# A hybrid decoder layer on one core: five read-in transfers for the RWKV-7 inverse, its steps tied to a large product, its way back by products with identity columns, and small edits at both ends of the program

## The chip, the cores and the metric

The kernel runs on one core of one Trainium2 chip. The core has a matrix engine (TensorE, in the profile PE, with its weight loads as PEld), three engines for elementwise work (VectorE or DVE, ScalarE or ACT, GpSimd or POOL) and SyncE (SP), whose queue here issues most transfers. A name that ends in q (SPq, ACTq) is the engine's queue, at work on waiting and issuing. Each engine takes its instructions strictly in the order in which the program lists them. The metric is the time of one execution in microseconds of device time, smaller is better. Times inside an execution are counted from the start of its span.

## What is computed

One layer of an inference step, in float32, for 256 new tokens of one prompt and one new token each of 8 sampled sequences, so 264 columns in all, with model width 2048:

```
x = x + 0.5 * swiglu(rmsnorm(x, n1), f1g, f1u, f1d)      # width 5504
proj = rmsnorm(x, nm) @ w_in                             # 2048 -> 1536 + 3328
o_att  = sliding-window attention, 16 query heads, 4 kv heads, sinks, relative bias
o_rwkv = RWKV-7 time mixing, 16 heads of 64
x = x + concat(o_att, o_rwkv) @ w_out
x = x + 0.5 * swiglu(rmsnorm(x, n2), f2g, f2u, f2d)
y = rmsnorm(x, final_norm)
```

The outputs are y, the new key and value windows, the RWKV state and the shift columns. The RWKV recurrence over the prompt's tokens, per head, is

```
sa = S @ (-kk);  S = S * exp(logw) + sa (kk*a)^T + v k^T;  y = S @ r
```

The kernel does not step through the tokens. It cuts them into chunks of 64, and inside a chunk the dependence of each token on the earlier ones is a strictly lower triangular 64x64 system. Its inverse is put together from two 32x32 blocks on the diagonal and one product for the block beside them. The 32x32 inverses are what the change is mostly about.

## The kernel before

**Activations and weights.** Activations lie with features on partitions and the 264 tokens as columns. Every weight is loaded from memory in float32 in pieces of 128x512 (`chunk`, L116). ACT rounds a piece to a short float (`hi`, L123), DVE computes the rest (`lo`, L124), and each 128x128 block takes three products, hi with hi, hi with lo and lo with hi (`gemm`, L127, `mm`, L73). A piece is thus twelve large products. There are six raw buffers and four each of `hi` and `lo`.

**Stages.** `first_ffn` (L284), then `mixing_body` (L337), then `second_ffn` (L912). The FFNs are almost nothing but large products. Mixing first multiplies by w_in, 38 output tiles (`win`, L374) of four pieces, then runs the output projection in three passes (`PASS`, L895) of 16 tiles. The small work of attention and RWKV is written as generators in a list `tasks`. After each piece of a large product, `tick` (L78) advances every task by one `yield`. I call that a chunk step. `pause(n)` lets n chunk steps go by. An output pass begins with `drain` (L83), which finishes the tasks that it needs.

**What orders the queues.** The order in which the program is written is a priority, not the final order. A planner with its own estimates of durations and transfers puts the instructions of each engine into their final order: among those that it believes ready, the earliest written goes first. Weight pieces of mixing have a raised priority. A buffer that is asked for again is given out once its last reader is done.

**The RWKV batches.** The 16 heads are 8 pairs, in four batches of two pairs (`BATCH`). `prep` (L401) computes per pair the masked products (`gm`), and sends their diagonal 32x32 blocks to a scratch in memory (`sa`, L488). When both pairs of a batch are there, `chain` (L527) goes on:

1. Read-in (L538 to L541): the 32 matrices of a batch, spread over 128 partitions with four partitions for each, come in as `X` (each matrix whole, four copies of it, one transfer a copy) and `Y` (named Xt in the profile, each partition a quarter of the rows, one transfer a quarter). Partition g*32+r holds copy g of matrix r. There is one buffer each.
2. `pause(DWAIT)`, eight steps, four for the last batch.
3. Thirty steps of substitution on DVE (L546 to L553), each a multiplication into `st` and an addition into Xt, with a `yield` after every fourth.
4. POOL fills ones into the diagonal (L555).
5. Way back: Xt is written to a second scratch `sb` (four transfers, L557) and from there read into `TT` (four transfers, L562) in the layout of the products.
6. `pause(DWAIT)` again, then two DVE transposes make `TN` from the first diagonal block of each half (L567).
7. Two sets of small products with a copy on ACT after each (`zs`, L579, `TT`, L588) make the block beside the diagonal. Then follow the products and copies that lead to the state and the output (`W` and `uv`, L602 to L604, and on).

One `yield` stands between the steps of 7. The tasks of attention (`attend`, L732) run in the same stage, with exponentials and table loads on ACT.

**Start.** `first_ffn` loads the first column block of x with the norm gains (`x0`), then one and two further blocks on the ACT queue, then four at a time. `NWARM` products of ones run on PE from the first microsecond. The first part multiplies all eight accumulators by the first four blocks of x before it goes on.

**End.** The sum of squares of the last rows comes from two half sums, each by small products into a PSUM tile of its own (L934 to L937). ACT copies one, DVE adds the other (L940, L941), then come root, reciprocal, and a product that spreads the factors over the partitions (L945), with five products that only keep PE busy in between (`hot`). ACT copies the result for POOL (L947), and DVE and POOL multiply the 16 output tiles in groups, each followed by its store (L948 to L952).

Of the kernel before, what the change touches and what calls it, by code (L numbers as in the profile page):

```python
# [7 lines left out]
F32 = mybir.dt.float32  # L8
# [5 lines left out]
P = 128  # L14
# [33 lines left out]
def body(tc, I, O):  # L48
    nc = tc.nc
    V, A, G, TE, SP = nc.vector, nc.scalar, nc.gpsimd, nc.tensor, nc.sync  # L50
    cnt = [0]

    def uid(s):
# [19 lines left out]
    def mm(out, lhsT, rhs, start=True, stop=True, **k):  # L73
        TE.matmul(out, lhsT, rhs, start=start, stop=stop, **k)  # L74

# [19 lines left out]
    with ExitStack() as ctx:  # L95
# [30 lines left out]

        def gemm(ps, src, xs, step=None, rng=None, ahead=True):  # L127
            n = len(xs)
            for k0 in range(0, n, CH):
                k1 = min(n, k0 + CH)  # L130
                if rng and k0 not in rng:
                    continue
                hi, lo = chunk(src[:, k0 * P:k1 * P], k1 - k0, V, ahead)
                for k in range(k0, k1):
                    xh, xl = xs[k]
                    c = slice((k - k0) * P, (k - k0 + 1) * P)
                    mm(ps[:, :T], hi[:, c], xh, k == 0, False)
                    mm(ps[:, :T], hi[:, c], xl, False, False)
                    mm(ps[:, :T], lo[:, c], xh, False, k == n - 1)
                if step:  # L140
                    step()
# [67 lines left out]

        def ffn(nrm, xr, gu, dn, nxt, load, begin=None, side=None):  # L210
            rstd = None
            f0 = 0
            for pi, nf in enumerate(PARTS):
# [5 lines left out]
                if first:  # L219
                    banks = [acc() for _ in range(NACC)] + [mp() for _ in range(NM)]  # L220
                    n0 = len(banks) // 2
                    for k in range(CH):
                        at = load(k)
                    for k0 in range(0, KD, CH):
                        if begin and k0 + CH < KD:
                            begin(k0 // CH + 1)
                        xs = nrm.xs + [None] * (KD - len(nrm.xs))
                        for i, ps in enumerate(banks):
                            with tc.issue_after(at.ins) if begin and k0 == 0 < i else nullcontext():
                                gemm(ps, gu[i // 2, i % 2], xs, rng=(k0,), ahead=False)  # L230
                            if i >= len(banks) - CH and k0 + CH < KD:
                                load(k0 + CH + i - len(banks) + CH)
# [51 lines left out]
        def first_ffn(n2):  # L284
# [8 lines left out]
            with tc.tile_pool(name="f1", bufs=1) as fp:  # L293
# [14 lines left out]

                ffn(n1, xr, I["gu1"], I["dn1"], nxt, load, more)

# [26 lines left out]
        def mixing_body(mx, n2, n3, XD, XR):  # L337
# [31 lines left out]
            scr = [dp.tile([BATCH[b] * 16, 1024], F32, tag=f"sa{b}", name=f"sa{b}") for b in range(nbat)]  # L369
            scr2 = [dp.tile([BATCH[b] * 16, 1024], F32, tag=f"sb{b}", name=f"sb{b}") for b in range(nbat)]  # L370
            mixed = [None] * 16
# [155 lines left out]
            def chain(bt):  # L527
# [4 lines left out]
                ng = P // nr  # L532
                if ng == 3:
                    ng = 2
                nj = 32 // ng
                X = ring((ng * nr, 32, 32), "X", 1)
                Y = ring((ng * nr, nj, 32), "Xt", 1)
                for g in range(ng):  # L538
                    SP.dma_start(X[g * nr:(g + 1) * nr], scr[bt.i].rearrange("r (s t) -> r s t", s=32))
                    SP.dma_start(Y[g * nr:(g + 1) * nr],  # L540
                                 scr[bt.i].rearrange("r (j g t) -> g r j t", g=ng, t=32)[g])  # L541
# [4 lines left out]
                for s in range(1, 31):  # L546
                    m, w = -(-s // ng), 31 - s
                    t = ring((ng * nr, m, w), "st", 2)
                    shp = (ng * nr, m, w)
                    tt(V, t, bc(X[:, s:s + 1, s + 1:], shp), bc(Y[:, :m, s:s + 1], shp), ALU.mult)  # L550
                    tt(V, Y[:, :m, s + 1:], Y[:, :m, s + 1:], t, ALU.add)
                    if s % NSTEP == 0:
                        yield  # L553
                for g in range(ng):
                    G.memset(Y[g * nr:(g + 1) * nr].rearrange("p j t -> p (j t)")[:, g:g + (nj - 1) * (32 + ng) + 1:32 + ng], 1.0)  # L555
                for g in range(ng):
                    SP.dma_start(scr2[bt.i].rearrange("r (j g t) -> g r j t", g=ng, t=32)[g], Y[g * nr:(g + 1) * nr])  # L557
                yield from pause(1)
                for h in range(2):
                    for blk in range(2):  # L560
                        x = h * 64 + blk * 32
                        SP.dma_start(TT[x:x + 32, :, blk * 32:blk * 32 + 32],  # L562
                                     scr2[bt.i].rearrange("(h b m) (s t) -> h b s m t", h=2, b=2, s=32)[h, blk])
                yield from pause(DWAIT[bt.i])
                TN = ring((P, n * 4, 32), "TN", 1)
                for h in range(2):
                    V.transpose(TN[h * 64:h * 64 + 32], TT[h * 64:h * 64 + 32, :, 0:32])  # L567
                yield
# [343 lines left out]
        def second_ffn(n3, xr, XR):  # L912
# [6 lines left out]
            with tc.tile_pool(name="f2", bufs=1) as fp:  # L919
# [13 lines left out]
                p = fin.sums[0]  # L933
                sm, rp, hot = [mp(), mp()], mp(), mp()  # L934
                for m, q in zip(sm, p):
                    for j in range(3):
                        mm(m[0:88, j:j + 1], q[:, j * 88:j * 88 + 88], ones[:, 0:1])  # L937
                for _ in range(5):
                    mm(hot[:, :P], ones, p[1][:, :P])
                A.copy(rt[:, 3:6], sm[0][0:88, 0:3])  # L940
                tt(V, rt[:, 0:3], sm[1][0:88, 0:3], rt[:, 3:6], ALU.add)  # L941
                act(rt[:, 0:3], rt[:, 0:3], AF.Sqrt, scale=1.0 / D, bias=eps[0:88, 0:1])
                V.reciprocal(rt[:, 0:3], rt[:, 0:3])
                for j in range(3):
                    mm(rp[:, j * 88:j * 88 + 88], bc(rt[:, j:j + 1], (88, P)), C[0:88, CID:CID + 88])  # L945
                rb = tmp()
                A.copy(rb, rp[:, :T])  # L947
                for i, (e, o, n) in enumerate(((V, 0, 1), (V, 1, 1), (G, 2, 1), (V, 4, 4), (G, 3, 1), (V, 8, 4), (G, 14, 1), (V, 12, 2), (V, 15, 1))):  # L948
                    y = ys[o // 4][:, o % 4:o % 4 + n]
# [112 lines left out]
```

## Time and profile before

| what | us |
|---|---|
| median of three runs | 2013.53 (2012.96 to 2017.21) |
| profiled execution, its own time | 2014.05 |
| its span | 2012.1 |
| first FFN at full rate, 69 to 761 | 692.00 |
| mixing, 760 to 1191 | 431.00 |
| second FFN, 1303 to 2000 | 697.00 |
| from the last large product to the end, 2000 to 2012.1 | 12.10 |

The profile is of one execution. Its span is what lies between the first and the last instruction, and its time is 1.95 us more. In the rows, `out<-in` names tiles with buffer numbers left out; `128x512 f32` is partitions by elements; `L74` is the line of the helper `mm`, so PE's groups are told apart by their tiles. A bracket `[5.00 <-DMA ...]` is the time that the engine sat idle before an instruction and what ended it. Where a wait has several semaphores, the one that came last is named, which need not be the cause. Each product in float32 appears as two PE instructions.

### The profile page before, as it was taken

What the parts mean: (1) busy time and instruction counts of PE and PEld (TensorE: products, weight loads), DVE (VectorE), ACT (ScalarE), POOL (GpSimd) and SP (SyncE); (2) the same over time, 40 slices, a digit from 0 to 9 for tenths busy, and PEclk for the clock granted to TensorE, in tenths of its full rate; (3) what the DMA queues carried; (4) which work ended last, traced back from release to release, by engine and by line L of the source; (5) the groups of instructions that cost most, each with busy time, mean ns of one, the idle gap of its engine ahead of it and who ended that gap; (6) DMA issues with size and microseconds to landing.
All of it is one profiled execution on the core that took longest, in us unless ns stands there. A gap on an engine that the chain in (4) does not pass through costs nothing.

```text
span 2012.1 us, 45443 instructions
## 1 busy us (share of the span) xinstructions
PE 1990.5 (99%) x17088; PEld 1956.4 (97%) x17088; DVE 1306.4 (65%) x2576; ACT 1032.6 (51%) x2047; POOL 257.0 (13%) x368
## 2 busy tenths in 40 slices
PE   9999999999999999999998999999999999999998
PEld 9999999999999999999988889999999999999998
DVE  5865555655556577688777766776666666666665
ACT  5644444444444456655555654654444444444445
POOL 0401001010010222121200010120101001010012
PEclk9999999999999999999999999999999999999999
DMA  6565565655555566554555345565565665655554
GB/s 226 177 192 193 183 194 189 185 184 176 187 177 185 182 200 211 153 157 129 149 150 165 118 137 181 174 184 184 192 179 191 187 192 189 185 191 184 191 179 145
DMA packets 227708, 358.39 MB, mean 178 GB/s; under 512 B 42384, under 2 KB 81312, under 8 KB 227488
## 3 DMA queue, kind: packets, MB, share of 16 engines
q1 hardware_dynamic: 220896, 346.41, 55.0%
q10 hardware_dynamic: 6592, 9.08, 1.4%
q8 instruction: 134, 2.20, 0.4%
q14 instruction: 86, 0.70, 0.1%
HBM read 347.26 MB, written 10.21 MB: 178 GB/s over the span
## 4 chain that ended last, share of the span: by engine, by line
PE 94%; DMA 2%; DVE 2%; issue 1%; ACT 1%; SPq 1%; DVEq 0%; POOL 0%; ACTq 0%; POOLq 0%
PE acc L74 85%; PE m L74 8%; DMA sb<-Xt 1%; DVE lo L58 0%; DMA TT<-sb 0%; DMA xsp<-x 0%; DMA x<-in_x 0%; DMA Xt<-sa 0%; PE m L507 0%; ACT t L68 0%; DVE y L58 0%; DMA sa<-gm 0%; SPq L557 0%; ACT hi L123 0%; PE m L757 0%
## 5 line engine op out<-in xcount | busy, mean ns | idle before, releaser
L58 DVE TENSOR_TENSOR lo<-raw,hi 128x512 fp32r<-128x512 f32 (+1 forms) x1288 | 871.2, 680 | 547.9 <-ACT hi L123 521.1
L123 ACT CAST hi<-raw 128x512 fp32r<-128x512 f32 (+1 forms) x1288 | 777.1, 607 | 840.9 <-PE acc L74 762.3
L74 PE MATMUL acc<-s,hi 128*128 128x264 f32 x5940 | 1112.0, 287 | 0.9 <-ACT hi L123 0.9
L74 PEld LDWEIGHTS acc<-s,hi 128*128 128x128 f32 x5940 | 924.2, 189 | 6.7 <-issue 1.9
L74 PE MATMUL acc<-s,lo 128*128 128x264 f32 x2970 | 848.9, 286 | 4.1 <-DVE lo L58 3.9
L74 PEld LDWEIGHTS acc<-s,lo 128*128 128x128 f32 x2970 | 560.3, 189 | 8.0 <-DVE lo L58 5.4
L74 PE MATMUL acc<-t,hi 128*128 128x264 f32 x2752 | 502.6, 284 | 0.0
L74 PEld LDWEIGHTS acc<-t,hi 128*128 128x128 f32 x2752 | 426.0, 188 | 0.0
L74 PE MATMUL acc<-t,lo 128*128 128x264 f32 x1376 | 388.6, 284 | 0.0
L58 POOL TENSOR_TENSOR t<-t,t 128x264 f32<-128x264 f32 (+1 forms) x148 | 150.9, 1020 | 1148.3 <-ACT hi L123 790.8
L74 PEld LDWEIGHTS acc<-t,lo 128*128 128x128 f32 x1376 | 258.3, 188 | 0.0
L74 PE MATMUL acc<-y,hi 128*128 128x264 f32 x648 | 123.7, 284 | 0.0
L74 PEld LDWEIGHTS acc<-y,hi 128*128 128x128 f32 x648 | 100.9, 188 | 0.1
L74 PE MATMUL acc<-y,lo 128*128 128x264 f32 x324 | 91.7, 283 | 0.0
L58 DVE TENSOR_TENSOR t<-acc,t 128x264 f32<-128x264 f32 x156 | 67.4, 432 | 36.8 <-PE acc L74 36.5
L58 POOL TENSOR_TENSOR o<-o,o 128x264 f32<-128x264 f32 x43 | 36.4, 847 | 234.6 <-ACT o L68 228.9
L74 PE MATMUL acc<-o,hi 128*128 128x264 f32 x324 | 63.1, 285 | 0.0
L74 PEld LDWEIGHTS acc<-y,lo 128*128 128x128 f32 x324 | 61.0, 188 | 0.0
L61 DVE SCALAR_TENSOR_TENSOR s<-acc,s 128x264 f32<-128x264 f32 x96 | 40.6, 427 | 15.4 <-PE acc L74 14.9
L74 PEld LDWEIGHTS acc<-o,hi 128*128 128x128 f32 x324 | 50.3, 188 | 0.0
L74 PE MATMUL m<-s,hi 128*128 128x264 f32 x260 | 48.0, 284 | 0.0
L61 DVE SCALAR_TENSOR_TENSOR x<-acc,x 128x264 f32<-128x264 f32 x96 | 40.5, 426 | 9.8 <-PE acc L74 9.3
(249 smaller groups left out, 1278.8 us busy)
## 6 DMA issues: line engine op xcount, KB each, us to landing
raw<-in_gu SPq DMA_DIRECT2D x688, 256.0 KB, 3.3
raw<-in_dn SPq DMA_DIRECT2D x224, 256.0 KB, 2.8
raw<-in_win SPq DMA_DIRECT2D x152, 256.0 KB, 3.4
raw<-in_dn SPq DMA_DIRECT2D x160, 192.0 KB, 2.7
raw<-in_wout SPq DMA_DIRECT2D x64, 256.0 KB, 3.2
xsp<-x ACTq DMA_DIRECT2D x16, 132.0 KB, 3.7
s<-xsp SPq DMA_DIRECT2D x16, 132.0 KB, 4.2
ld<-in_sT SPq DMA_DIRECT2D x16, 128.0 KB, 3.5
```

The source lines that it names most:

```text
L58: return e.tensor_tensor(out=out, in0=a, in1=b, op=op)
L61: return V.scalar_tensor_tensor(out=out, in0=a, scalar=s, in1=b, op0=op0, op1=op1)
L74: TE.matmul(out, lhsT, rhs, start=start, stop=stop, **k)
L123: A.copy(hi[:, :w], raw[:, :w])
```

## The change

The read-in of `X` becomes one transfer that repeats each matrix four times, so that partition 4*r+g holds matrix r; the four transfers of `Y` write every fourth partition accordingly. `DWAIT` becomes ten steps, eight for the last batch. The first substitution step gets a dependence, for the planner only, on the last large product written before it. The fill of the diagonal, the second scratch and its eight transfers go. Instead, eight steps after the substitution, 32 small products per batch multiply columns of `Y` as the stationary operand with columns picked from the identity, and so bring each 32x32 inverse to the partitions where it is needed; DVE adds the unit matrix on the way out of PSUM into `TN`, which now holds all four blocks, and makes `TT`'s two diagonal blocks by four transposes.

At the start, one more warm product; the first weight piece is written ahead of the second to fourth block of x, and the transfer with the third and fourth goes to SP's queue. At the end, both half sums accumulate in one PSUM tile, the root reads it directly, three products keep PE busy instead of five, the spreading product is done twice so that ACT's copy has a tile of its own, and the output tiles are grouped and shared between DVE and POOL in another way.

```diff
-NWARM = 10
+NWARM = 11
-DWAIT = (8,8,8,4)
+DWAIT = (10,10,10,8)
...
     def mm(out, lhsT, rhs, start=True, stop=True, **k):
-        TE.matmul(out, lhsT, rhs, start=start, stop=stop, **k)
+        return TE.matmul(out, lhsT, rhs, start=start, stop=stop, **k)
+
+    def behind(i):
+        tc.add_manual_dep(i.ins, big[0].ins.name, mybir.DependencyInfo(mybir.DependencyClass.NoSync, mybir.DependencyReason.SCHED_ONLY))
+        return i
...
-                hi, lo = chunk(src[:, k0 * P:k1 * P], k1 - k0, V, ahead)
+                hi, lo = ready or chunk(src[:, k0 * P:k1 * P], k1 - k0, V, ahead)
...
-                    mm(ps[:, :T], lo[:, c], xh, False, k == n - 1)
+                    big[0] = mm(ps[:, :T], lo[:, c], xh, False, k == n - 1)
...
-                for j0, j1 in ((1, 2), (2, 4)):
+                at = load(0)
+                with tc.issue_after(at.ins):
+                    first = chunk(I["gu1"][0, 0][:, 0:CH * P], CH, V, False)
+                for e, j0, j1 in ((A, 1, 2), (SP, 2, 4)):
                     xg = fp.tile([P, j1 - j0, T], F32, name=uid("x"))
-                    A.dma_start(xg, I["xT"][:, j0:j1, :])
+                    e.dma_start(xg, I["xT"][:, j0:j1, :])
...
+            unit = fix((P, 32), "unit")
+            for i in range(4):
+                G.tensor_copy(unit[i * 32:i * 32 + 32, :], ident[i * 32:i * 32 + 32, i * 32:i * 32 + 32])
...
+                SP.dma_start(X.rearrange("p s t -> p (s t)"), bc(scr[bt.i].unsqueeze(1), (nr, ng, 1024)))
                 for g in range(ng):
-                    SP.dma_start(X[g * nr:(g + 1) * nr], scr[bt.i].rearrange("r (s t) -> r s t", s=32))
-                    SP.dma_start(Y[g * nr:(g + 1) * nr],
+                    SP.dma_start(Y.rearrange("(r g) j t -> g r j t", g=ng)[g],
                                  scr[bt.i].rearrange("r (j g t) -> g r j t", g=ng, t=32)[g])
...
-                    tt(V, t, bc(X[:, s:s + 1, s + 1:], shp), bc(Y[:, :m, s:s + 1], shp), ALU.mult)
+                    keep = behind if s == 1 else lambda i: i
+                    keep(tt(V, t, bc(X[:, s:s + 1, s + 1:], shp), bc(Y[:, :m, s:s + 1], shp), ALU.mult))
...
-                for g in range(ng):
-                    G.memset(Y[g * nr:(g + 1) * nr].rearrange("p j t -> p (j t)")[:, g:g + (nj - 1) * (32 + ng) + 1:32 + ng], 1.0)
-                for g in range(ng):
-                    SP.dma_start(scr2[bt.i].rearrange("r (j g t) -> g r j t", g=ng, t=32)[g], Y[g * nr:(g + 1) * nr])
-                yield from pause(1)
-                for h in range(2):
+                yield from pause(8)
+                ps = mp()
+                cols = ident.rearrange("p (h b m g) -> p g h b m", g=ng, h=2, b=2)
+                for j in range(nj):
                     for blk in range(2):
+                        for h in range(2):
+                            x = h * 64 + blk * 32
+                            mm(ps[x:x + 32, j * ng * n * 4:(j + 1) * ng * n * 4], Y[:, j, :], cols[:, :, h, blk, :])
+                TN = ring((P, n * 4, 32), "TN", 1)
+                tt(V, TN, ps[:, :32 * n * 4].rearrange("p (s m) -> p m s", m=n * 4), bc(unit.unsqueeze(1), (P, n * 4, 32)), ALU.add)
+                yield
+                for blk in range(2):
+                    for h in range(2):
                         x = h * 64 + blk * 32
-                        SP.dma_start(TT[x:x + 32, :, blk * 32:blk * 32 + 32],
-                                     scr2[bt.i].rearrange("(h b m) (s t) -> h b s m t", h=2, b=2, s=32)[h, blk])
-                yield from pause(DWAIT[bt.i])
-                TN = ring((P, n * 4, 32), "TN", 1)
-                for h in range(2):
-                    V.transpose(TN[h * 64:h * 64 + 32], TT[h * 64:h * 64 + 32, :, 0:32])
+                        V.transpose(TT[x:x + 32, :, blk * 32:blk * 32 + 32], TN[x:x + 32])
...
-                sm, rp, hot = [mp(), mp()], mp(), mp()
-                for m, q in zip(sm, p):
+                sm, rp, hot = mp(), mp(), mp()
+                for i, q in enumerate(p):
                     for j in range(3):
-                        mm(m[0:88, j:j + 1], q[:, j * 88:j * 88 + 88], ones[:, 0:1])
-                for _ in range(5):
+                        mm(sm[0:88, j:j + 1], q[:, j * 88:j * 88 + 88], ones[:, 0:1], i + j == 0, i == 1, skip_group_check=True)
+                for _ in range(3):
                     mm(hot[:, :P], ones, p[1][:, :P])
-                A.copy(rt[:, 3:6], sm[0][0:88, 0:3])
-                tt(V, rt[:, 0:3], sm[1][0:88, 0:3], rt[:, 3:6], ALU.add)
-                act(rt[:, 0:3], rt[:, 0:3], AF.Sqrt, scale=1.0 / D, bias=eps[0:88, 0:1])
+                act(rt[:, 0:3], sm[0:88, 0:3], AF.Sqrt, scale=1.0 / D, bias=eps[0:88, 0:1])
...
-                rb = tmp()
-                A.copy(rb, rp[:, :T])
-                for i, (e, o, n) in enumerate(((V, 0, 1), (V, 1, 1), (G, 2, 1), (V, 4, 4), (G, 3, 1), (V, 8, 4), (G, 14, 1), (V, 12, 2), (V, 15, 1))):
+                rb, again = tmp(), mp()
+                for j in range(3):
+                    mm(again[:, j * 88:j * 88 + 88], bc(rt[:, j:j + 1], (88, P)), C[0:88, CID:CID + 88])
+                A.copy(rb, again[:, :T])
+                for i, (e, o, n) in enumerate(((V, 0, 1), (V, 1, 1), (V, 2, 2), (V, 4, 4), (G, 8, 1), (V, 9, 3), (G, 12, 1), (V, 13, 3))):
```

More of the change, by code (lines that the diff above doesn't have):

```diff
@@ L51, in body @@
     cnt = [0]
+    big = [None]
     def uid(s):
@@ L125, in chunk, with gemm @@
             return hi, lo
-        def gemm(ps, src, xs, step=None, rng=None, ahead=True):
+        def gemm(ps, src, xs, step=None, rng=None, ahead=True, ready=None):
             n = len(xs)
@@ L208, in copy_one, with ffn @@
             tc.keep_in_program_order(A.dma_start(O[n][b, 0:127, :], I[c][b, 1:128, :]))
-        def ffn(nrm, xr, gu, dn, nxt, load, begin=None, side=None):
+        def ffn(nrm, xr, gu, dn, nxt, load, begin=None, side=None, ready=None):
             rstd = None
@@ L221, in ffn @@
                     n0 = len(banks) // 2
-                    for k in range(CH):
+                    for k in range(len(nrm.xs), CH):
                         at = load(k)
@@ L229, in ffn @@
                             with tc.issue_after(at.ins) if begin and k0 == 0 < i else nullcontext():
-                                gemm(ps, gu[i // 2, i % 2], xs, rng=(k0,), ahead=False)
+                                gemm(ps, gu[i // 2, i % 2], xs, rng=(k0,), ahead=False, ready=ready)
+                            ready = None
                             if i >= len(banks) - CH and k0 + CH < KD:
@@ L307, in more @@
                     xr.extend(xg[:, j] for j in range(4))
-                ffn(n1, xr, I["gu1"], I["dn1"], nxt, load, more)
+                ffn(n1, xr, I["gu1"], I["dn1"], nxt, load, more, None, first)
         def dec_state(fp, XR):
@@ L369, in mixing_body @@
             scr = [dp.tile([BATCH[b] * 16, 1024], F32, tag=f"sa{b}", name=f"sa{b}") for b in range(nbat)]
-            scr2 = [dp.tile([BATCH[b] * 16, 1024], F32, tag=f"sb{b}", name=f"sb{b}") for b in range(nbat)]
             mixed = [None] * 16
@@ L532, in chain @@
                 ng = P // nr
-                if ng == 3:
-                    ng = 2
                 nj = 32 // ng
```

## The prediction

> **What bounds the kernel now.** I read the page's engine totals first, then busy time by stage, and then who waits for whom inside the one stage that the change rewrites.
>
> ```profile
> span 2012.1 us, 45443 instructions
> PE 1990.5 (99%) x17088; PEld 1956.4 (97%) x17088; DVE 1306.4 (65%) x2576; ACT 1032.6 (51%) x2047; POOL 257.0 (13%) x368
> ```
> ```profile
> 69.00:761.00 692.00, 692.00 (x5693) 691.94 (x5692) 415.16 (x703) 339.14 (x610) 88.27 (x86) 1.00 0.59 187
> 760.00:1191.00 431.00, 420.98 (x4248) 388.48 (x4248) 319.30 (x889) 252.02 (x639) 66.73 (x168) 0.99 0.52 150
> 1303.00:2000.00 697.00, 696.96 (x5719) 696.85 (x5717) 444.13 (x769) 342.27 (x613) 83.41 (x88) 1.00 0.59 184
> ```
>
> TensorE bounds everything: 692.00 of 692.00 us in the first FFN, 696.96 of 697.00 in the second (columns: stretch, length, then PE, PEld, DVE, ACT, POOL with counts). Nothing in the change touches those two. What can move lies in the first 15 us, in the mixing stage (760 to 1191), where PE misses 10.0 us of 431.00 and DVE is busy 74% (319.30), and in the last 12 us. A product added in mixing costs its full time; a wait removed gains only what PE itself lost. That loss is small and is listed here, the waits of PE in the mixing stage (total, times, longest, us):
>
> ```profile
> PE acc L74 <- DVE lo L58: 3.9, 3, 2.2
> PE m L74 <- ACT zs L579: 3.5, 1, 3.5
> PE m L74 <- ACT W L602: 1.4, 1, 1.4
> PE m L74 <- DVE TN L567: 0.5, 1, 0.5
> ```
>
> **Which of these the read-in and the way back cause.** The timelines of DVE and PE, and the chain of waits (start, length, what), show the three large ones:
>
> ```profile
> 853.52 0.19 DVE L58 TENSOR_TENSOR st<-X,Xt 128x30 f32<-128x30 f32 x1 [5.00 <-DMA raw<-in_win]
> 1033.76 0.43 DVE L567 STREAM_TRANSPOSE TN<-TT 32x256 f32<-32x256 f32 x1 [2.47 <-DMA TT<-sb]
> 1036.28 0.44 DVE L567 STREAM_TRANSPOSE TN<-TT 32x256 f32<-32x256 f32 x1 [1.44 <-DMA TT<-sb]
> 1060.16 0.19 DVE L58 TENSOR_TENSOR st<-X,Xt 128x30 f32<-128x30 f32 x1 [5.00 <-DMA out_vp<-s]
> ```
> ```profile
> 848.74 4.60 DMA Xt<-sa
> 896.29 0.60 SPq L557
> 1033.08 3.17 DMA TT<-sb
> ```
> ```profile
> 858.06 0.39 PE L74 MATMUL acc<-s,lo 128*128 128x264 f32 x1 [1.49 <-DVE lo L58]
> 1037.83 0.40 PE L74 MATMUL acc<-s,lo 128*128 128x264 f32 x1 [2.20 <-DVE lo L58]
> 1064.24 0.33 PE L74 MATMUL m<-BT,W 64*64 64x64 f32 x4 [1.38 <-ACT W L602]
> ```
>
> DVE stands 5.00 us before the first substitution step of batch 0, because the last Xt transfer lands 4.60 us after 848.74 (the name in the bracket is only the semaphore that fired last); the weight split `lo` queued behind it is late and PE loses 1.49. At 1033 to 1036 DVE waits twice for the transfers that bring the inverse back, and PE loses 2.20. At 1055 to 1060 DVE waits 5.00 for batch 3's X and Xt, the copy of `uv` behind it delays ACT's `W` of batch 2, and PE loses 1.38. With the 0.5 on `TN` that is 5.6 us. The remaining large one, 3.5 on `zs`, is ACT's own queue and has no transfer in it.
>
> **The change, part by part.**
>
> *Way back by products.* Removed per batch: four writes to sb, four reads into TT, four POOL fills, two DVE transposes. Added per batch: 8 x 2 x 2 = 32 float32 products, all 128 rows by 32 columns, 32 columns moved. A float32 product is two PE instructions here, so 64. The nearest rows, PE's timeline:
>
> ```profile
> 990.49 1.15 PE L74 MATMUL m<-uv,BT 128*64 128x64 f32 x32
> 991.47 1.10 PE L74 MATMUL m<-gm,uv 128*64 128x64 f32 x32
> 1050.24 0.69 PE L74 MATMUL m<-TN,gm 32*32 32x32 f32 x32
> 1050.86 0.39 PE L74 MATMUL acc<-s,hi 128*128 128x264 f32 x1
> 1169.22 0.96 PE L74 MATMUL m<-t,ld 128*128 128x8 f32 x8
> 1170.04 0.37 PE L74 MATMUL acc<-s,hi 128*128 128x264 f32 x1
> ```
>
> From start to next start: 32 instructions of 32 columns take 0.62 us, 19.4 ns each; 32 of 64 columns with all 128 rows take 0.98, 30.6 ns. I take 19.4, since the moved width is the same: 64 x 19.4 = 1.24 us, times four batches +5.0 us, all of it on the path. Upper end 30.6 ns: +7.8. The third pair is what a bare weight load looks like: 8 instructions that load 128 columns and move only 8 take 0.82, 102 ns each, 0.8 ns a loaded column. If 32-column loads stood bare too, they would add 26 ns each, 256 x 26 = +6.6 us; that is the price of a rival below. The lower end is 0 where PE would have stood anyway.
>
> The Trainium skill, "TensorE: Matmul & The Clock Gate", Part 3 on packing small matmuls, says that a weight load overlaps running products only when its row group differs. These products use all rows, so by that rule their loads lie bare, against the change. The trace disagrees where it can be asked: `m<-uv,BT` uses all 128 rows, loads 64 columns, and takes 30.6 ns, less than a bare load of 64 columns (51 ns by the 0.8 above). By the row the sum gets +5.0, by the rule +11.6.
>
> *DVE.* Its groups in the mixing stage:
>
> ```profile
> L567 DVE STREAM_TRANSPOSE TN<-TT 32x256 f32<-32x256 f32 x8 | 3.5, 434 | 11.0 <-DMA TT<-sb 10.9
> L58 DVE TENSOR_TENSOR t<-m,t 128x264 f32<-128x264 f32 x8 | 3.4, 423 | 0.0
> ```
>
> The four POOL copies that build `unit` stand at the start of mixing, on an engine that is 15% busy there (66.73 of 431.00): 0. On DVE come four transposes for two, and one addition of `unit` read from PSUM: 2 x 0.434 + 0.42 = +1.3 us a batch, +5.2 in all, in an engine that is idle a quarter of the stage and loses up to 10.9 + 3 x 5 us of waiting. Cost on the path 0 while DVE is on time. The new chain has two more handovers a batch (products to addition to `TN`, transposes to `TT`), queued one chunk step apart. Twelve such handovers of today (`zs`, `TT`, `W` in four batches) cost 1.4 without the odd 3.5, 0.12 each; 8 x 0.12 = +1.0 us. Ends: 0, and 1.5 a batch (a rival).
>
> *Read-in by five transfers, later steps.* The SP queue's issues, by tile (min, median, max ns; first and last start, us):
>
> ```profile
> L539 SPq DMA_DIRECT2D X<-sa x16: 316/595/1057, 843.6 to 1054.9; - x16
> L540 SPq DMA_DIRECT2D Xt<-sa x16: 543/553/665, 844.0 to 1056.0; - x16
> ```
>
> Eight issues (4 x 0.60 + 4 x 0.55 = 4.6 us, with weight transfers among them) become one of about 0.6 and four of 0.55, 2.8 us; bytes and piece sizes stay. The last landing comes 1.8 us or more earlier. Beginning the substitution ten chunk steps after the read-in instead of eight, and in the planner's order behind a big product, covers the rest of batch 0's 5.00. SP also loses 8 issues a batch and its wait for sb's landing; weight transfers queued behind them only gain. Xt is released later, by the products instead of by the write. The next batch asks for it one chunk step before the products are emitted, so its Xt transfers wait a step or so, with weight transfers behind them in SP's queue; six weight buffers, one a step, cover that: 0. I count all 5.6 us as gone; lower bound 0.5, if only the `TN` wait goes.
>
> *Later last batch.* Batch 3 had 4+1+4 pauses and has 8+8: about eight steps later in program order, still some 16 steps ahead of the second output pass, which drains it: 0.
>
> *Start.* ACT and PE now:
>
> ```profile
> 7.95 0.51 ACT L68 ACTIVATE s<-x,x 128x264 fp32r<-128x264 f32 x1 [1.02 <-DMA x<-in_xT]
> 6.56 6.93 PE acc L74 x26
> 13.73 1.23 PE acc L74 x10
> ```
>
> The third and fourth x tiles wait 1.02 us for a transfer third in ACT's queue; from SP's second place it lands about 1 us earlier. PE's gaps around it shrink by some 0.6 us while products still start every 0.22 us (6.93 less some 1.2 of gaps, over 26), before they go to 1.23/10 = 0.12: three more products done, -0.4 us. The eleventh warm product ends at about 5.8, before 6.56: 0. One extra issue ahead of SP's second weight chunk (0.4 us) hides behind twelve products of the first.
>
> *End.*
>
> ```profile
> 2001.10 1.36 PE L74 MATMUL m<-o,ones 128*128 128x128 f32 x10
> 2001.34 0.16 DVE L58 TENSOR_TENSOR rt<-m,rt 88x3 f32<-88x3 f32 x1 [1.30 <-PE m L74]
> 2002.30 0.80 PE L74 MATMUL m<-C,rt 88*128 88x88 f32 x6
> 2003.13 0.38 ACT L947 COPY t<-m 128x264 f32<-128x264 f32 x1 [1.30 <-PE m L74]
> 2003.54 4.05 DVE L58 TENSOR_TENSOR y<-y,m 128x264 f32<-128x264 f32 x6 [1.51 <-ACT t L947]
> ```
>
> Without the `rt` addition (0.2 with its handover) and four of ten heating instructions (0.5, which hold `m<-C,rt` until 2002.30) the broadcast starts about 0.4 earlier; with its own copy `again` for ACT, DVE no longer stands the 0.41 from 2003.13 to 2003.54. DVE then multiplies 14 tiles instead of 13 (+0.3), and the last transfer is three tiles instead of one. -0.8 at the start of the stores, -0.6 at the end.
>
> *Sum* against the profiled 2014.05 us (span 2012.1 and 1.95 around it): +5.0 +1.0 -5.6 -0.4 -0.6 = -0.6. That profile lies 0.5 above the median 2013.53; the forecast on the median is 2012.9.
>
> **Rivals.**
> - *The read-in is not better covered (no change).* The big product behind which batch 3 begins is fixed in program order; the last X is issued only at 1054.9. For: the wait was shorter than its cover, yet there. Then 1.38 stays: 2014.3.
> - *The rate doubles earlier.* With fewer gaps after 6.56, PE's step from 0.22 to 0.12 may come halfway, 3.4 us earlier, 15 products at 0.10 less: -1.5, 2011.4. The Trainium skill, "TensorE: Matmul & The Clock Gate", Part 1, says that full rate needs a busy window and that windows run free of the kernel; this profile shows one start only.
> - *ACT's wait goes too (faster).* These two queues collided once:
>
> ```profile
> 1094.32 1.28 ACT L68 ACT_TABLE_LOAD   x1 [0.88 <-DVE sta L65]
> 1097.87 0.75 ACT L579 COPY zs<-m 32x256 f32<-32x256 f32 x2
> ```
>
> `zs` of batch 3 stood behind a table load and softmax work. Batch 3 now reaches it at another moment, without about 9 us of transfers. For: one wait in four batches. Against: its steps move deeper into the attention tasks. 2012.9 - 3.5 = 2009.4, over the line with any other gain.
> - *DVE is late for the products (slower).* PE takes its queue in order, so products planned before Y is done hold all that follows. Weight transfers mark the chunk steps, one each:
>
> ```profile
> L122 SPq DMA_DIRECT2D raw<-in_win x152: 327/328/1296, 754.7 to 1074.5; - x152
> ```
>
> That is 152 in 320 us, 2.1 a step, so eight steps of substitution and eight of pause are 34 us. Batch 0's sixty operations now last from 853.52 to the first write at 896.29, 42 us. At 1.5 a batch, the loss of 858.06: +6.0, 2018.9; beyond 1.2 a batch it is slower by my bound. Against: the planner places products when it thinks Y done.
> - *Bare weight loads (slower).* +6.6: 2019.5. Against: the rows above.
>
> **How the numbers follow.** Forecast 0.32, read-in not covered 0.07, rate earlier 0.09, ACT's wait gone 0.31, DVE late 0.14, bare loads 0.07. I take 0.2% (4 us) as what a measurement here can tell from no change: faster 0.31, same 0.48, slower 0.21. Likeliest 2012.9, alone 2009.6 to 2016.5. The range of 2006.5 to 2019.0 takes in the ACT case with an earlier rate and half of the slow ones.
>
> **What would show it.** DVE's wait before `st` under 1 us in all batches and no sb or TT transfers; 64 instructions `m<-Xt,C` a batch in 1.2 to 2.0 us; PE waits on `lo` in mixing under 1 us; first store issue near 2003.2 if PE ends where it did. Wrong if PE waits before `m<-Xt,C` or for `TN`, if the products take over 2 us a batch, or if `zs` decides.

## The result and the profile after

The changed kernel takes 1999.03 us (median of 4 runs, 1997.15 to 2001.78) beside 2013.24 (4 runs, 2008.44 to 2017.21): 0.993 of the time, 95% interval 0.9908 to 0.9952. The forecast was 2012.9 with a range of 2006.5 to 2019.0. The profiled execution took 2000.26 us.

The page of the changed kernel: span, engine totals, and the first line of the chain that ended last, in which PE had 94% before. The second fence has its stretches, as those shown of before (start and end, length, busy time of PE, PEld, DVE, ACT, POOL with counts, granted clock, DMA share, GB/s).

```profile
span 1998.5 us, 45869 instructions
PE 1987.7 (99%) x17348; PEld 1956.4 (98%) x17348; DVE 1313.3 (66%) x2587; ACT 1032.5 (52%) x2046; POOL 253.8 (13%) x355
...
PE 99%; DVE 0%; DMA 0%; issue 0%; ACT 0%; DVEq 0%; ACTq 0%
```
```profile
66.00:758.00 692.00, 692.00 (x5693) 691.90 (x5691) 415.13 (x702) 339.01 (x610) 88.31 (x86) 1.00 0.60 187
757.00:1180.00 423.00, 422.91 (x4512) 392.71 (x4511) 328.17 (x905) 253.27 (x643) 65.61 (x157) 0.99 0.49 151
```

The first FFN is the same 692.00 us. In mixing, PE is busy 422.91 of 423.00 us, where it missed 10.0 of 431.00. These are all waits of PE in the whole changed program (total, times, longest, us); none lies in mixing:

```profile
PE m L75 <- POOL eps L155: 1.0, 1, 1.0
PE acc L75 <- ACT hi L128: 0.7, 1, 0.7
PE m L75 <- ACT o L69: 0.6, 1, 0.6
PE acc L75 <- DVE lo L59: 0.2, 1, 0.2
```

To place the gain in this pair of executions I set the same large product (hi or lo with an activation, counted from the start) of both traces side by side. No. 30 starts 2.76 us earlier, no. 6240 (start of mixing) 2.82, no. 8784 (after mixing) 11.64, no. 14975 (the last) 13.04, and the span ends 13.65 earlier. So between these two executions the start differs by 2.8, mixing by 8.8, the second FFN by 1.4, the end by 0.6. What other executions do is told with the runs below.

Mixing, from no. 6240 to no. 8784, splits as follows. "Clock" is PE's busy time times what the granted clock lacks to 1.00, over windows of 1 us; "identity" the products with identity columns, from the first to the start of what follows.

| us | length | PE idle | clock | identity | rest |
|---|---|---|---|---|---|
| before | 473.79 | 10.02 | 3.36 | 0 | 460.41 |
| changed | 464.97 | 0.09 | 3.41 | 4.33 | 457.14 |
| way back alone (e4) | 477.73 | 9.15 | 6.76 | 2.77 | 459.04 |
| later steps alone (e5) | 469.69 | 6.07 | 4.75 | 0 | 458.86 |
| all edits of mixing (e3) | 460.25 | 0.00 | 0.00 | 4.52 | 455.73 |
| last run (e16) | 459.93 | 1.53 | 1.71 | 2.77 | 453.91 |

### The profile page after: what moved, and what is told of

Same layout as the page of the kernel before. It is cut to its first block, busy times and chain, and to the rows that moved or that the text cites. A ratio compares the mean times of both kernels' runs of the same rounds, so it can differ in the third digit from the quotient of the medians.

```text
span 1998.5 us, 45869 instructions
## 1 busy us (share of the span) xinstructions
PE 1987.7 (99%) x17348; PEld 1956.4 (98%) x17348; DVE 1313.3 (66%) x2587; ACT 1032.5 (52%) x2046; POOL 253.8 (13%) x355
## 4 chain that ended last, share of the span: by engine, by line
PE 99%; DVE 0%; DMA 0%; issue 0%; ACT 0%; DVEq 0%; ACTq 0%
PE acc L75 89%; PE m L75 9%; PE m L518 0%; DMA x<-in_x 0%; DVE y L59 0%; PE m L768 0%; PE m L466 0%; PE m L505 0%; PE m L770 0%; PE m L769 0%; PE m L715 0%; DVE lo L59 0%; DVE t L704 0%; ACT hi L128 0%; ACT s L69 0%
```

## The experiments

**The parts one by one (e1 to e4).** Each is the kernel before with one group of edits of the diff.

```diff
 e1_start: NWARM 11; first weight piece ahead of x; x blocks 3 and 4 on SP
 e2_end:   one `sm` tile, three `hot`, `again`, new groups of `y`
 e3_mix:   all edits of mixing (read-in, DWAIT, behind, way back)
 e4_wayback: the products, `unit` and transposes for scr2, with the old read-in and old DWAIT
```


> Before with the start of the change alone: eleven warm products, the first weight piece written ahead of x, the transfer of the third and fourth x tiles on SP's queue. Theory G (PE's rate doubles one step earlier because PE hardly stands between the warm products and the first real ones): -2 to -3 us, and in the profile products start every 0.12 us from about 7 us on instead of 13.3. Theory X (only the transfer's gap goes, as predicted): -0.4 us, the rate still doubles at about 13.

> Before with the end of the change alone. Both theories: -0.6 us, DVE's first final multiplication about 0.9 us sooner after the last large product than before, mixing and start unchanged (-0.3 to -0.9).

> Before with all edits of the mixing stage, start and end as before. Theory W (the waits of PE in mixing, 9.5 us in the profile of before, all go, zs included, and the products cost 3.7): -6 to -9 us, PE waits in mixing under 0.5. Theory C (the wait for zs went by chance with another order, and start and end made the rest): -2 us, a wait of PE on ACT of 1 us or more somewhere in mixing.

> Before with only the way back replaced: old read-in of eight transfers in blocks of partitions, old pauses before the substitution, no tie to a large product; the products, addition and four transposes of the change. Theory W: the waits on TN go (2.7 us of PE) and 3.7 us of products come, so +1 us (-1 to +3); DVE's wait of 5 us before the substitution stays in batches 0 and 3 with PE losing 1 to 2 us behind each. Theory B (the transfers of the way back cost more than PE's named waits, since the whole chain moves): -4 us or better.

Beside 2014.65 us of before: start 2011.85 (ratio 0.9988, interval 0.9974 to 1.0001), end 2012.56 (0.9987, 0.9977 to 0.9997), mixing 1999.37 (0.9921, 0.9907 to 0.9936), way back alone 2017.03 (1.001, 1.0001 to 1.0019). The gain is in mixing: e3, without the edits of start and end, has the ratio of the whole change (0.993, and 0.9927 in e15 below), so the times do not show that start and end add anything to it. The part that I had costed most closely is slower by itself. DVE's and PE's timelines of e4 show why:

```profile
966.49 1.80 DVE L568 STREAM_TRANSPOSE TT<-TN 32x256 f32<-32x256 f32 x4
977.10 0.19 DVE L58 TENSOR_TENSOR st<-X,Xt 128x30 f32<-128x30 f32 x1 [8.82 <-DMA Xt<-sa]
```
```profile
985.42 0.48 PE L74 MATMUL m<-BT,W 64*64 64x64 f32 x4 [5.80 <-ACT W L603]
```

Batch 2's read-in is issued from 969.9 on, just after the last of its own writes to `sa` has landed (969.8). With eight pauses its first step stands early in DVE's queue and holds it for 8.82 us; DVE's copies of `uv` are behind it, ACT's next `W` behind those, and PE loses 5.80. It is not the late release of Xt that holds this read-in: batch 1's products were done with Xt at 965.5. In all 18 profiles the first transfer of `X` goes out 0.0 to 1.1 us after the batch's last write to `sa` has landed.

**Which of mixing's parts (e5 to e8).** e5 is before with the pauses and the tie alone; the others are the changed kernel with one part taken back.

```diff
 e5_steps:    before, DWAIT = (10,10,10,8), behind()
 e6_oldread:  changed, X and Xt by eight transfers, cols = "p (g h b m) -> p g h b m"
 e7_oldsteps: changed, DWAIT = (8,8,8,4), no behind()
 e8_nobehind: changed, no behind()
```


> The kernel before with only the later steps: ten pauses for eight (eight for four in the last batch) and the tie of the first substitution step to a large product; eight-transfer read-in and way back through memory stay. Theory C (the cover of the read-in is what counts): DVE's waits of 5.0 us before `st` in batches 0 and 3 go, PE's wait of 1.5 on `lo` near 858 and the 1.4 on `W` go, and so may `zs` by moving batch 3 by eight steps; the waits on TT's transfers stay with PE's 2.2: some 3 to 7 us less than before, 2008 to 2011 beside 2014.6. Theory D (the three parts only work together, since the way back through memory sets the rest): PE still loses 8 us or more in mixing, the time within 2 us of before.

> The changed kernel with the old read-in: X and Xt by eight transfers, each to a block of 32 partitions, and the products' identity columns picked to match. All else as changed. If the cover by ten steps and the tie is enough, 4.6 us of issues on SP in place of 2.8 make nothing late: PE loses under 1 us in mixing, the time within 1.5 us of 1999.0. If the five transfers are what takes the waits away, DVE waits 2 to 5 us before `st` again and PE loses 3 us or more: 2002 to 2006.

> The changed kernel with the old pauses (eight, four in the last batch) and without the tie; five-transfer read-in and products stay. If the pauses carry the gain, DVE waits before `st` for Xt again (some 3 us in batch 0, 3 to 5 in batch 3), PE loses 3 to 9 us in mixing: 2002 to 2008. If read-in and products carry it: within 1.5 us of 1999.0 and PE's idle time in mixing under 1 us.

> The changed kernel without the tie of the first substitution step to a large product; ten pauses and all else stay. If the pauses alone cover the read-in: within 1 us of 1999.0, DVE's waits before `st` 3 us or less. If the tie does it: the first step goes ahead of weight splits in DVE's queue, DVE waits 3 to 5 us before `st`, PE loses 1.5 to 5 us on `lo`: 2000.5 to 2004.

Beside 2012.77 of before: later steps alone 2007.12 (0.997, 0.9959 to 0.9981); old read-in 1998.88 (0.9923, 0.9899 to 0.9948); old pauses 2003.33 (0.9948, 0.9928 to 0.9969); no tie 1997.56 (0.9923, 0.9901 to 0.9945). So beside the new pauses and the products, neither the five transfers nor the tie show a gain. With the old pauses it is not so: e7 differs from e4 by the five transfers and by the edits of start and end, and its ratio is 0.9948 where that of e4 is 1.001, some 12 us, of which start and end had 5 by their medians (e1, e2). DVE's waits before `st` fall from 21.7 us in e4 to 12.9 in e7. The largest waits of PE in mixing, of e5 and then of e7:

```profile
PE m L75 <- DVE TN L574: 2.2, 2, 1.2
PE acc L75 <- DVE lo L59: 1.2, 2, 0.9
PE m L75 <- ACT W L609: 1.0, 1, 1.0
```
```profile
PE m L75 <- ACT W L613: 2.5, 2, 1.9
PE m L75 <- DVE N L59: 0.9, 1, 0.9
PE m L75 <- DVE S L62: 0.5, 1, 0.5
```

With the pauses alone, DVE still waits for the way back (5.0 us before `TN`, for the transfers into TT). With the products and the old pauses, DVE waits for Xt before `st` (these 12.9 us, in four waits) and `W` is late; with the longer pauses the 7.9 us of such waits in e8 cost PE nothing. The pauses alone gave 5.7 us, the products alone cost 2.4, both together with the rest of mixing's edits gave 15.3. One reason may lie in the starts of the batches; it is argued here and no run tests it alone. In before, batch 3's read-in is issued from 1050.3 on, its first step runs at 1060.2 and its `zs` products at 1098.3; in the changed kernel the three stand at 1026.9, 1034.7 and 1094.8. The last batch has 60 us for its chain in place of 38. Since each read-in starts when the batch's `sa` has landed (batch 3: 1050.2 and 1026.9), it is `prep` that comes earlier; why it does is not shown.

**The price of the products (e9, e10).**

```diff
 e9_double:   the loop over j, blk, h stands twice
 e10_samecol: for blk: for h: for j   (in place of for j: for blk: for h)
```


> The changed kernel with its 32 products with identity columns done twice in each batch (the second set writes the same values over the first), 64 more PE instructions a batch. If the products lie on PE's path at the 14 ns that the changed kernel's profile shows, four more sets cost 4 x 64 x 14 ns = 3.6 us: 2002.6 beside 1999.0; at the prediction's 19.4 ns 2004.0; if PE had room for them, no change.

> The changed kernel with the products in another order: the eight of one quarter of the output partitions behind one another, in place of a new quarter with each product. Same products, same sums. If the 14 ns come from neighbours that go to different quarters of the array and run side by side, a set takes 19 to 30 ns an instruction now, 1.2 to 1.9 us a batch in place of 0.9, and the kernel 1.3 to 4 us more: 2000.3 to 2003. If the order does not matter: 0.9 us a batch and 1999.0.

PE's timelines of the changed kernel, of e10 and of e16 (below), a set of products with what follows it:

```profile
894.07 1.15 PE L75 MATMUL m<-C,Xt 128*32 128x32 f32 x64
895.15 0.71 PE L75 MATMUL m<-ld,tw 65*128 65x128 f32 x4
```
```profile
893.74 3.26 PE L75 MATMUL m<-C,Xt 128*32 128x32 f32 x64
896.92 0.71 PE L75 MATMUL m<-ld,tw 65*128 65x128 f32 x4
```
```profile
892.87 0.76 PE L75 MATMUL m<-C,Xt 128*32 128x32 f32 x64
893.56 0.71 PE L75 MATMUL m<-ld,tw 65*128 65x128 f32 x4
```

A set takes 1.08 us (16.9 ns an instruction, not the 14 that I first read from the changed trace), 4.3 us in the kernel. Done twice it takes 2.06, and the time rises from 1999.03 to 2000.17: 1.1 us where 3.9 of PE time were added. The profiled mixing is 2.9 longer; the ranges of the two kernels overlap (e9: 1998.0 to 2001.52), so the median is a poor measure here. In the order of e10 a set takes 3.18 us, 49.8 ns an instruction, and the kernel 2006.92: 7.9 more, where 4 x (3.18 - 1.08) = 8.4 were to come. The single records agree: in the changed kernel four instructions start within 30 ns and the next four 33 to 41 ns later. In e10 they start 50 to 60 ns apart, and only around the three changes of quarter do pairs start within 17 ns; the two products of such a pair have different stationary columns, so it is not shared columns that let them run together. So instructions that write different quarters of the output partitions run side by side, weight loads included; to the same quarter they follow one another. How much of the 33 ns between the two is weight load is not separated. The Trainium skill, "TensorE: Matmul & The Clock Gate", Part 3, has a sentence on each: its column tiling, by which outputs at 32-partition steps run together, agrees with 16.9 against 49.8 ns. Its sentence that loads overlap only across row groups does not fit these loads of all 128 rows.

**The clock behind a wait (e11, e13, e14) and the start (e12).**

```diff
 e11_zsdve: before; batch 3's zs copied by DVE in place of ACT
 e12_xsp:   before; order of transfers at the start as changed, NWARM 10
 e13_hot3:  before; batch 3, after the zs copies:
+                if bt.i == 3:
+                    hot = mp()
+                    mm(hot[0:32, 0:P], ident[0:32, 0:32], TN[0:32, 0:4, :])
+                    for _ in range(12):
+                        mm(hot[:, 0:P], ident, ident)
 e14_late3: before; DWAIT = (8,8,8,8)
```


> The kernel before with one edit: batch 3's copy of `zs` out of PSUM is done by DVE in place of ACT, so that it does not stand behind ACT's softmax work. Theory W (a wait costs its own length): PE's 3.5 us of idle go, the time is 3.5 less, 2010 beside 2013.5. Theory K (the idle also halves the granted clock for some 7 us behind it, which costs 3.4 more): the clock stays at 1.00 through 1092 to 1110, the time is about 7 less, 2006.5. If another wait takes its place, PE's idle time in mixing stays near 10 us and the time at 2013.

> The kernel before with only the other order of transfers at the start (first weight piece ahead of the x blocks, the third and fourth x block on SP's queue); ten warm products stay. If the earlier x is what lets PE's rate double before 8 us, the 30th large product starts 2.5 to 3 us earlier than before and the time is 2 us less, as in the run with both edits of the start. If the eleventh warm product is needed, it starts within 1 us of before.

> The kernel before with 13 float32 products that nothing reads (26 PE instructions, at the 0.136 us of `m<-o,ones` some 3.5 us), put in PE's queue between `m<-TN,gm` and `m<-TT,zs` of batch 3, where PE stands 3.5 us. The order of all else is that of before. Theory W (a wait costs its own length): the wait is only filled, the time stays, 2012.5 to 2014. Theory K (a wait of that length also halves the granted clock for the 7 us behind it): the clock stays at 1.00 from 1092 to 1108, and the time is 3 to 3.5 us less, 2009 to 2010.

> The kernel before with eight pauses in place of four in the last batch, twice, and nothing else. If the 3.5 us on `zs` come from where batch 3 stands against ACT's softmax work, they go with this alone, and with them the low clock behind them: 2007 to 2009. If they need the later steps of the other batches too, PE loses about 10 us in mixing as before: 2012 to 2014.

The stretches of before around PE's wait on `zs`, then those of e13 (granted clock is the third number from the end):

```profile
1092.50:1096.00 3.50, 2.34 (x46) 1.79 (x44) 3.44 (x9) 2.29 (x3) 0.36 (x1) 1.00 0.89 238
1096.00:1099.50 3.50, 1.06 (x32) 0.95 (x32) 3.17 (x16) 2.58 (x12) 0.23 (x1) 0.88 0.97 264
1099.50:1103.00 3.50, 3.50 (x32) 3.04 (x28) 1.44 (x8) 3.18 (x12) 0.00 (x0) 0.50 1.08 365
1103.00:1106.50 3.50, 3.50 (x30) 3.17 (x28) 1.74 (x6) 3.49 (x16) 0.74 (x1) 0.64 0.75 234
```
```profile
1089.00:1092.50 3.50, 1.97 (x43) 1.46 (x41) 3.44 (x9) 2.59 (x5) 0.59 (x1) 1.00 0.83 230
1092.50:1096.00 3.50, 3.22 (x20) 3.02 (x21) 2.81 (x15) 3.44 (x15) 0.00 (x0) 0.76 0.96 316
1096.00:1099.50 3.50, 3.50 (x51) 3.02 (x49) 1.46 (x5) 3.21 (x13) 0.75 (x1) 0.75 1.03 346
1099.50:1103.00 3.50, 3.50 (x35) 3.07 (x35) 3.09 (x12) 2.61 (x9) 1.66 (x2) 1.00 0.48 145
```

e13 takes 2011.12 beside 2013.86 (0.9988, 0.9979 to 0.9997): 26 instructions whose result nobody reads make the kernel faster by 2.7 us, with an interval of 0.6 to 4.2. That the wait costs only its own length does not fit: filled, it would have left the time as it was. The profile alone does not show that the clock is the reason. A wait of 1.8 on `y` stands ahead of the filler there, one low stretch of 3.4 us remains of the two, and another of 3.4 comes at 1183, so that the clock is low for 6.8 us of mixing, as in before; and of the 4.9 us by which this execution is shorter, 3.9 were there ahead of the filler (`m<-TN,gm` of batch 3 stands at 1090.28, in before at 1094.14). Nor is the order behind the filler quite that of before: three large products now stand ahead of `m<-kr,TT`. What speaks for the clock is the mean granted clock on record for every run. What it lacks to 1.00, times the span, averages 10.4 us in before (21 runs) and 7.9 in e13 (11 runs), 2.5 less, near the 2.7 of the times. e11 settles nothing, since DVE's queue was as full there as ACT's: PE still waited 3.3 us on `zs` and the time was 2013.88 (1.0008, 0.9998 to 1.0017). e14 is slower, 2015.93 (1.0014, 1.0005 to 1.0024). With the last batch alone moved, no wait on `zs` is left, but PE waits 7.6 us on `y` and on tiles of the attention shortly before 1097, 1101 and 1105 instead, 14.1 us idle in all, and the clock is low for 17.1 us from 1097 on. (Its profiled execution was its longest, 2021.97.) The wait on `zs` is also gone in e4 and in e5, with either half of the edits of mixing alone.

e12, in the windows of 1 us at the start: before, then e12. The clock column says nothing here, since the trace of before holds no clock record ahead of 13.23 us; the number of instructions does.

```profile
8.00:9.00 1.00, 1.00 (x4) 0.51 (x3) 0.50 (x2) 1.00 (x3) 0.00 (x0) 1.00 0.99 338
9.00:10.00 1.00, 1.00 (x5) 0.96 (x5) 0.99 (x2) 1.00 (x3) 0.00 (x0) 1.00 0.80 221
```
```profile
8.00:9.00 1.00, 1.00 (x10) 1.00 (x9) 1.00 (x4) 1.00 (x3) 0.00 (x0) 1.00 1.08 418
9.00:10.00 1.00, 1.00 (x11) 1.00 (x10) 1.00 (x3) 0.83 (x2) 0.00 (x0) 1.00 0.98 375
```

PE does 10 instructions a microsecond from 8 us on, where before did 4 to 7 until 13: the order of the transfers alone brings the full rate 5 us earlier, without the eleventh warm product, and no. 30 starts 2.75 us earlier. All profiles agree: in the ten kernels with this order of transfers full clock is granted from 4.7 to 6.9 us on and stays; in the eight without, it comes for good only at 11.8 to 14.0, and six of these had it for 3.4 us from about 5 on and lost it again. Yet the time is 2012.54, that of before (1.0003, 0.9991 to 1.0016): in that execution mixing took 475.21 us, 1.4 more, with 2.3 us of waits on ACT's `s` that before did not have. In the changed kernel's profile the 2.8 us stay to the end, but e3, which has the old start and the old end, is no slower. So an earlier start of 2.8 us is shown, and a shorter time from it is not.

**Without the two parts that show no gain of their own (e15, e16).**

```diff
 e15_again: the changed kernel
 e16_best:  changed, old read-in by eight transfers (as e6), no behind()
```


> The changed kernel as it is, beside the next one on the same chip: 1997 to 2001.

> The changed kernel with the old block-wise read-in by eight transfers and without the tie; pauses, products, start and end as changed. Its products take 10.8 ns an instruction in place of 16.9 (the identity columns lie side by side), 4 x 64 x 6.1 ns = 1.6 us less. If that is all that the two parts do, 1.6 us less than the changed kernel beside it, 1997.4. If the tie or the five transfers save waits in some executions, it is no faster.

Beside 2013.86 of before, the changed kernel took 1998.62 (0.9927, 0.9914 to 0.9939; 1996.79 to 2001.64), e16 1995.32 (0.9906, 0.9891 to 0.9922; 1993.46 to 1995.76): the fastest of all, 3.3 us below the changed kernel. With the block-wise read-in the identity columns that one product moves lie side by side, and a set takes 0.69 us in place of 1.08 (third fence of the products above), 1.6 us in four batches. The other 1.7 are not explained by a run.

## Why the prediction was wrong

*Waits (-5.6 predicted): the step that failed.* The waits were read one by one, each with its cause, and 5.6 of the 9.3 us listed were taken as gone. All of them went: PE's idle time in mixing fell by 9.9 us. I had set `zs` (3.5) apart because it was "ACT's own queue and has no transfer in it"; its rival had 0.31. As far as the runs show, that wait hung on when batch 3 reached ACT's softmax work, as the rival had it. The products alone (e4) remove it and so do the later steps alone (e5): the read-in of batch 3 starts 5 and 10 us earlier there, its `zs` products run 4 to 5 us later, and other waits take its place. Only together do they leave PE without waits (e3). The rival's mechanism happened. Its price was too small, since it was added to a sum that left the rest of mixing as it was.

*Clock: no term at all.* Behind the wait on `zs` the granted clock is halved, which cost before 3.4 us in its profile (e13 gives 2.7 for filling the wait). In the profiled changed execution the same 3.4 are lost at another place. In the stretch ahead of it PE is never idle, but most of its instructions are from products that move 8 columns:

```profile
1166.00:1169.50 3.50, 3.50 (x31) 2.90 (x31) 0.00 (x0) 0.37 (x1) 0.00 (x0) 1.00 0.48 148
1169.50:1173.00 3.50, 3.50 (x20) 3.50 (x18) 1.08 (x5) 1.01 (x3) 0.54 (x5) 0.50 0.02 5
1173.00:1176.50 3.50, 3.50 (x14) 2.51 (x14) 2.03 (x3) 1.29 (x4) 2.46 (x7) 0.52 0.23 70
```

That stretch is not in every execution (none in the profiles of e3, e8 and e10), so the pair of profiles hides what the clock is worth. By the mean granted clock of every run, what it lacks to 1.00 times the span averages 10.8 us in before (25 runs) and 5.5 in e3 (4 runs), which has the start and the end of before; the changed kernel has 5.6 (e15, 5 runs) beside 10.4. By this estimate (a run's clock is given to 0.001, 2 us) some 5 of the 15 us are clock. The forecast needed this term and had none.

*Products (+5.0)*: the path was right, the size off: 16.9 ns an instruction instead of 19.4, +4.3. The loads of the rival did not stand bare; in the order of e10 an instruction takes 33 ns more, where the rival had 26 for a load.

*New handovers (+1.0)*: 0. DVE stood 3.6 us for the products before `TN`, PE never for DVE. DVE late for the products (rival): no.

*Read-in*: the wait on Xt did not fall under 1 us in all batches as I had said; batch 3 still has one of 3.0 at 1034.66, and PE loses nothing by it. The rival, by which PE's 1.4 on `W` stays when the read-in is no better covered, did not happen either: with the old eight transfers (e6) PE lost nothing.

*Late release of Xt (0)*: the cost was right. In the changed kernel the Xt transfers of batches 1 to 3 do wait for it, 1.6 to 4.6 us behind X, and PE loses nothing. That the six weight buffers cover this, as I had said, is not shown. In e4 it holds batch 1's Xt by some 3 us, but 8.2 of PE's 8.9 us of waits on `W` there come behind the read-ins of batches 2 and 3, where it holds nothing.

*Later last batch (0)*: by itself +2.1 (e14); it is of use only with the other edits.

*Start (-0.4)*: -2.8 at the 30th large product, and no gain shown in the time. The rival "the rate doubles earlier" is what happened, at one and a half times its price (-0.4 and -1.5), because the rate doubled at about 7.5 us and not halfway to 13.7. It was not weighed high enough: the trace of before showed products at 0.22 us for 6.9 us after a start with gaps, and with the other order of transfers the early full clock stayed in ten profiles of ten.

*End (-0.6)*: -0.6 between the two profiles; from the last large product, DVE's first multiplication comes 3.44 us later in place of 4.25, -0.8 as worked out.

*What no term had*: the rest of mixing fell by 3.3 us in groups that did not change, the largest being `m<-t,s` (12.1 to 11.0 us, and to 10.4 without its half clock). What makes them shorter I cannot separate. Three groups that look shorter too (`m<-kr,TT` 9.3 to 8.2, `m<-s,o` 10.7 to 9.6, `m<-TT,zs` 3.4 to 2.8) ran partly at half clock in before, which the column "clock" already counts. The second FFN's 1.4 is no effect of the change that I can show: across all 18 profiles it lies between 752.4 and 755.8 us, in kernels with and without each edit. The sum, -2.8 (start) - 9.9 (idle) + 0.1 (clock) + 4.3 (products) - 3.3 (rest) - 1.4 (second FFN) - 0.6 (end) = -13.6, is the difference of the two spans.

## What to carry to other kernels

Waits of the bounding engine in one stage are not independent terms: where several tasks share in-order queues, edits that come together can take all of them away, and an edit that shortens or moves one link can lengthen the stage (e4, e14) until its partner comes too. So give "all of them go" its own case, priced at the whole idle time plus the low clock behind the waits, and read the clock from all runs and not from one profile. Small products are priced by the order of their outputs and by the spacing of what they move: the same 32 products took 0.69, 1.08 or 3.18 us.

## What the runs showed of the hardware

- The granted clock fell to 0.50 in stretches of about 3.4 us, each worth 1.7 us: the losses in mixing of the profiles without long waits are 0, 1.71, 3.41 and 5.13. They came behind idle times of PE (3.5 us in before, 5.8 in e4, 3.3 in e11), but also behind shorter ones (1.8 in e13, 1.9 in e7, and 10.2 us of low clock behind waits of 1.0 and 1.2 in e5), and without any idle, behind 128x8 products (1169.5 in the changed kernel). A wait of 2.4 us at 1058 in e4 brought none, so the length of a wait alone does not decide. The Trainium skill, "TensorE: Matmul & The Clock Gate", Part 1, states half rate after an idle window of some 3.4 us; the three long ones come near to it, and that sentence does not cover the others.
- Filling a wait of 3.5 us on PE with useless products saved 2.7 us (0.6 to 4.2; e13). The mean granted clock of the runs makes 2.5 of it, as an estimate.
- With identity columns spaced four apart an instruction of 32 moved columns took 16.9 ns, side by side 10.8 (e16).
